# An encoder's instruction planner with a transfer rate of 280 bytes per ns, without table loads in its costs, and with every fifth low part made by GpSimd

## The chip, the cores and the metric

The kernel runs on one core of a Trainium2 chip. The metric is the device time of one launch, in microseconds, as the median of several runs. The engines of the core are TensorE (PE; PEld is its loading of weights), VectorE (DVE), ScalarE (ACT), GpSimd (POOL) and SyncE (SP), which issues nearly all transfers. Each engine executes its own row of instructions in order; semaphores hold an instruction until what it needs is there.

## The reference

Two layers of an encoder over 256 tokens of width 1024, everything in fp32. A layer has four branches, each 256 wide, that are computed from the same normed input, gated, merged and projected, and then a SwiGLU feed-forward part with 2816 hidden columns:

```python
def hybrid_layer(x, mem, ...):
    h = rms_norm(x, norm_mix_g)
    proj = h @ w_in                                   # 1024 x 2304
    rq, rk, rv, rg, pv, nq, nk, nv, mq = jnp.split(proj, 9, axis=-1)
    ret = ...      # retention of rq, rk, rv with rotary and decay both ways, per-head norm, silu(rg)
    pool = ...     # centred means of pv over 2, 4, 8, 16 positions, minus pv, a map per group
    na = ...       # attention of nq, nk, nv in a 2-D window, with bias and normed q and k
    mk, mv = jnp.split(rms_norm(mem, norm_mem_g) @ w_mem_kv, 2, axis=-1)
    mo = ...       # attention of mq to the 256 memory tokens, with normed q and k
    branches = jnp.stack([ret, pool, na, mo], axis=2)
    up = jnp.einsum('bsnc,ncd->bsnd', branches, w_branch)
    gates = jax.nn.sigmoid(h @ w_gate).reshape(b, s, N_BRANCH, dm)
    x = x + jnp.einsum('bsnd,bsnd->bsd', gates, up) @ w_out
    a, g = jnp.split(rms_norm(x, norm_ffn_g) @ w_ffn_in, 2, axis=-1)
    return x + (jax.nn.silu(a) * g) @ w_ffn_out
```

## The kernel before

**Weights.** All weights of both layers are read once, as a stream of 272 slots of 128 x 1024 fp32 (512 KB): per layer 18 for w_in, 4 for the memory's keys and values, 32 for the gates, 8 for the branch projections, 8 for w_out, 44 for the first and 22 for the second feed-forward matrix. A slot j lands in one of four raw buffers (RAW, NR = 4). To keep fp32 precision, it is split in two: the high part whi (ten buffers, NS = 10) is a cast of raw to fp32r by ScalarE, and the low part wlo (ten buffers too) is raw minus whi by VectorE. The activations are split in the same way (hhi and hlo from the normed input, bhi and blo from branches and feed-forward). Each product is then three matmuls on PE: high by high, high by low, low by high. The slots are used in order, each by both token tiles (t = 0 and 1, 128 tokens each), into the PSUM banks A0 to A3 and B0, B1. Banks C0 and C1 (B0 and B1 too in the branches) serve transposes, attention scores and other small steps.

**Transfers.** `issue_dmas` keeps up to four slots under way beyond the number of low parts that have been put in the program; SyncE issues them. So a low part, once placed, is followed in the program by the issue of the slot that reuses its raw buffer.

**The order.** The kernel's rows are not written out by hand. `tile_encoder` runs a planner: each engine is wrapped by `Engine`, whose `call` enters every instruction in a model, `Clock`, before it goes into the program. `Clock.cost` gives an instruction's duration, `Clock.enter` when it starts and ends in the model, transfers included. At each step the planner takes the model's time of PE as now. `background` resumes the chains of small steps (norms, heads, attention, gates, feed-forward's silu: each a Python generator) as soon as what they need is there in the model; `soon`, `ready`, `there`, `need` and `acquire` ask the model's times. `pump` places the casts (`split_hi`) and the low parts (`split_lo`) when the engine is free soon and the transfer has landed in the model, with a window that shrinks with the number of low parts placed ahead of use, WINDOW = (6, 4, 1.5, 0.4) us. `emit` places the matmuls of one slot for one token tile. So a number in the model changes the order of the rows and with it nothing else: what an instruction takes on the chip is not in the program. The first four slots are placed by hand (`begin`).

**The stretches of a layer.** w_in, then four branches in the order neighbourhood attention (2), memory attention (3), retention (0) and pooling (1), each with its 8 gate slots and 2 projection slots; then w_out, then the feed-forward part. `branch_chain` is the one long chain through the four branches: it turns queries and keys into heads (`to_heads`, bank C), computes scores (bank B), the exponentials with their sums (sc, sums), scales, turns and multiplies by the values, while PE works on gate and projection matmuls in between. `ev_nqk` and `ev_mem` norm the heads of queries and keys from the PSUM banks; their reciprocal root is a power on GpSimd of a few elements (sm, rms), otherwise GpSimd has two memsets.

ScalarE computes sigmoids (gates, silu) and exponentials (attention); where one follows the other, a table load stands in its row. VectorE's products of the feed-forward part read `w<-A,rms,w`: bank A, the token's norm, the sigmoid in w.

Nearly every instruction carries the line of the helper that enters it in the model, line 61, so the rows are told apart by tiles. The numbers behind a tile's name in the order's rows are those of buffers.

Of the kernel before, what the change touches and what calls it, by code (L numbers as in the profile page):

```python
# [9 lines left out]
F32 = mybir.dt.float32  # L10
# [20 lines left out]

NS = 10
NR = 4
LEAD = 7
MAX_LAG = 8
WARM = 6.6
TABLE_LOAD = 1.28
WINDOW = (6, 4, 1.5, 0.4)
VERBOSE = False
BRANCHES = (2, 3, 0, 1)  # L40
# [3 lines left out]
class Engine:  # L44
# [5 lines left out]
    def __getattr__(self, op):  # L50
        f = getattr(self.real, op)

        def call(*args, **kw):
            outs = [kw[k] for k in ("out", "accum_out") if kw.get(k) is not None]
            ins = [v for k, v in kw.items() if k not in ("out", "accum_out")]
            rest = list(args)
            if "out" not in kw:
                outs.append(rest.pop(0))
            func = next((v for v in rest if isinstance(v, AF)), None)
            self.clock.enter(self.name, op, outs, [v for v in ins + rest if isinstance(v, bass.AP)], kw, func)  # L60
            return f(*args, **kw)  # L61

        return call


class Clock:
# [5 lines left out]
    def __init__(self):  # L72
        self.at = dict.fromkeys(("PE", "ACT", "DVE", "POOL", "SP", "DMA"), 0.6)
        self.reads, self.writes = {}, {}
        self.mark = 0.0
        self.column = None
        self.narrow = False
        self.table = None

    @property  # L80
    def now(self):
# [2 lines left out]
    def cost(self, eng, op, outs, ins, kw):  # L84
        n = max([x.free_size() for x in outs[-1:] + ins[:1]])
        if eng == "PE":
            o = outs[0]
            n = o.free_size() * (2 if self.now < WARM else 1)
            narrow = op == "matmul" and ins[0].dtype == F32 and o.partition_size() == HD
            change = 0.2 * (narrow != self.narrow)  # L90
            self.narrow = narrow
            if op == "transpose":
                return n * 0.845e-3 + change
            if ins[0].dtype == F32R:
                return n * 0.4167e-3 + 0.0135 + change
            half = o.partition_size() == HD and o.base_partition()
            if o.partition_size() == HD:
                pair, self.column = self.column, None if half else n
                if half and pair == n:
                    return 0.02  # L100
            return max(n, 128) * 1.67e-3 + change
        if eng == "ACT":
            return 0.1 + n * 0.83e-3 + 0.1 * (kw.get("accum_out") is not None) + 0.04 * isinstance(kw.get("scale"), bass.AP)
        if eng == "POOL":
            if op == "memset":
                return 0.1 + n * 1e-3
            return 0.3 + 0.17 * n
        if op in ("tensor_copy", "tensor_scalar", "tensor_scalar_mul", "tensor_scalar_add", "memset"):
            return 0.085 + n * 0.6e-3
        return 0.08 + n * 1.045e-3 + 0.05 * (op == "scalar_tensor_tensor")  # L110

    def span(self, x):
        (stride, parts), *free = x.ap
# [12 lines left out]
        old = [r for r in table.get(key, ()) if r[4] > end - 60 and not (p0 <= r[0] and r[1] <= p1 and lo <= r[2] and r[3] <= hi)]  # L126
        table[key] = old + [(p0, p1, lo, hi, end, eng)]

    def enter(self, eng, op, outs, ins, kw, func=None):
        ins = [x for x in ins if x.space != bass.MemoryType.DRAM]  # L130
        outs = [x for x in outs if x.space != bass.MemoryType.DRAM]
        skip = "PE" if eng == "PE" else None
        t = max([self.last(self.writes, x) + self.LATENCY for x in ins]
                + [self.last(self.reads, x, eng) + self.LATENCY for x in ins if x.space == bass.MemoryType.PSUM]
                + [max(self.last(self.writes, x, skip), self.last(self.reads, x, skip)) + self.LATENCY for x in outs] + [self.at[eng]])
        if func in (AF.Exp, AF.Sigmoid) and func != self.table:
            self.table = func
            self.at["ACT"] += TABLE_LOAD
            t = max(t, self.at["ACT"])
        if op == "dma_start":  # L140
            self.at[eng] = t + 0.45
            t = max(self.at["DMA"], t + 1.2) + (outs + ins)[0].nbytes() / 390e3
            self.at["DMA"] = t
            end = t + 1.0
        else:
            end = self.at[eng] = t + self.cost(eng, op, outs, ins, kw)
        for x in ins:
            self.note(self.reads, x, end, eng)
        for x in outs:
            self.note(self.writes, x, end, eng)  # L150
        self.mark = max(self.mark, end)
# [9 lines left out]
def tile_encoder(ctx: ExitStack, tc: tile.TileContext, a: dict, out: bass.AP):  # L161
# [129 lines left out]
    def split_lo():  # L291
        j = state["lo"]
        for o in HALVES if j < 3 else [slice(None)]:
            nc.vector.tensor_sub(WLO[j % NS][:, o], RAW[j % NR][:, o], WHI[j % NS][:, o].bitcast(F32))
        state["lo"] += 1
        issue_dmas()

    def soon(t, slack=0.4):
        return t <= clock.now + slack

    def pump():
# [5 lines left out]
            window = min(window, 0.8)  # L307
        for _ in range(2):
            j = state["lo"]
            if j < state["hi"] and soon(clock.at["DVE"], window) and soon(clock.last(clock.writes, WHI[j % NS])):  # L310
                split_lo()
            j = state["hi"]
            if (j < min(n_slots, state["free"] + NS, state["lo"] + NR) and soon(clock.at["ACT"], window)
# [868 lines left out]
```

## Time and profile before

| | us |
|---|---|
| runs shown: lowest, median, highest | 842.88, 843.17, 847.2 |
| the profiled execution, whole | 841.89 |
| its span in the trace | 840.0 |
| PE busy | 820.8 |
| VectorE busy | 552.2 |
| ScalarE busy | 470.1 |
| GpSimd busy | 30.5 |

The profiled execution's 841.89 us is its own device time, comparable with the runs; the span of 840.0 is what the trace covers of it, 1.9 less. PE's mean granted clock was 1.00. Stretches of the span, by what PE works on: the start up to about 16 us; the first layer's w_in, gates and branches to about 180; the merge, w_out and the way to the feed-forward part to 265; the feed-forward part to 425; then layer two in the same way, up to 590, 680 and 840. A row of busy time has the engine's share of the span behind it; a row of a wait gives the waiting engine and tile, what released it, microseconds, count and the longest; and a row of the trace has the start in us, the duration in us, the engine, line, operation and operands, and in brackets the idle time ahead of it and what ended that.

### The profile page before, as it was taken

The numbers are of one execution on the slowest core, as the hardware profiler recorded it, in microseconds if no ns is written. First come the engines' busy times: TensorE is split into PE (matmuls) and PEld (weight loads), VectorE is DVE, ScalarE is ACT, GpSimd is POOL, SyncE is SP. The second block draws the span as 40 slices with busy tenths as digits, with TensorE's granted clock in tenths as the row PEclk, the third lists the DMA queues.
The fourth block names the chain that finished last, engine by engine and source line by source line (L and its number), as shares of the span: only waits on it lengthen the run. The fifth ranks groups of instructions, "written<-read, shape, count | busy, mean of one in ns | idle before, by whom it ended". The sixth has DMA issues, their size and how long they took to land.

```text
span 840.0 us, 10795 instructions
## 1 busy us (share of the span) xinstructions
PE 820.8 (98%) x3928; PEld 672.4 (80%) x3928; DVE 552.2 (66%) x802; ACT 470.1 (56%) x726; POOL 30.5 (4%) x32
## 2 busy tenths in 40 slices
PE   8999999999999999999999998999999999999998
PEld 6788778778887888888888877887888878888886
DVE  5898786865677556555568868584775765655541
ACT  6858887445465444444469677754444654444430
POOL 0400100000000000000011001000000000000000
PEclk9999999999999999999999999999999999999999
DMA  8946765546568656566374477446544676666611
GB/s 257 323 140 203 240 199 166 166 147 197 176 180 255 191 180 197 176 198 185 95 220 137 156 246 219 147 126 226 178 157 120 200 228 198 187 187 186 189 52 51
DMA packets 103765, 152.86 MB, mean 182 GB/s; under 512 B 6432, under 2 KB 55328, under 8 KB 103712
## 3 DMA queue, kind: packets, MB, share of 16 engines
q1 hardware_dynamic: 102848, 151.30, 57.1%
q10 hardware_dynamic: 864, 0.88, 0.3%
q8 instruction: 31, 0.51, 0.2%
q14 instruction: 22, 0.18, 0.1%
HBM read 151.10 MB, written 1.05 MB: 181 GB/s over the span
## 4 chain that ended last, share of the span: by engine, by line
PE 78%; ACT 7%; DMA 7%; DVE 6%; issue 2%; POOL 0%; SPq 0%; DVEq 0%; ACTq 0%; POOLq 0%
PE A L61 49%; PE B L61 25%; PE C L61 4%; DVE wlo L61 3%; ACT whi L61 2%; DMA raw<-in_w_in 2%; DMA mem<-in_pool_a 2%; DMA raw<-in_w_ffn_out 1%; DMA raw<-in_w_gate 1%; DVE w L61 1%; ACT rs L61 1%; ACT sc L61 1%; DMA raw<-in_w_mem_kv 1%; ACT qk L61 1%; ACT bhi L61 1%
## 5 line engine op out<-in xcount | busy, mean ns | idle before, releaser
L61 DVE TENSOR_TENSOR wlo<-raw,whi 128x1024 fp32r<-128x1024 f32 (+1 forms) x275 | 330.2, 1212 | 190.9 <-ACT whi L61 190.3
L61 ACT CAST whi<-raw 128x1024 fp32r<-128x1024 f32 (+1 forms) x273 | 284.1, 1050 | 214.0 <-PE A L61 83.0
L61 PE MATMUL A<-whi,hhi 128*128 128x512 f32 (+1 forms) x544 | 213.9, 393 | 1.6 <-ACT whi L61 0.7
L61 PE MATMUL A<-wlo,hhi 128*128 128x512 f32 (+1 forms) x544 | 208.9, 384 | 1.0 <-DVE wlo L61 1.0
L61 PE MATMUL A<-whi,hlo 128*128 128x512 f32 (+1 forms) x544 | 209.1, 384 | 0.0
L61 PEld LDWEIGHTS A<-whi,hhi 128*128 128x128 f32 x544 | 102.3, 188 | 23.2 <-issue 2.6
L61 PEld LDWEIGHTS A<-whi,hlo 128*128 128x128 f32 x544 | 102.2, 188 | 21.2 <-DVE hlo L61 0.8
L61 PEld LDWEIGHTS A<-wlo,hhi 128*128 128x128 f32 x544 | 102.5, 188 | 20.1 <-DVE wlo L61 2.0
L61 PE MATMUL B<-whi,hlo 128*128 128x512 f32 x288 | 112.5, 391 | 0.1
L61 PE MATMUL B<-whi,hhi 128*128 128x512 f32 x288 | 112.3, 390 | 0.0
L61 PE MATMUL B<-wlo,hhi 128*128 128x512 f32 x288 | 112.1, 389 | 0.0
L61 PE MATMUL A<-whi,bhi 128*128 128x512 f32 x272 | 108.3, 398 | 0.0
L61 PE MATMUL A<-whi,blo 128*128 128x512 f32 x272 | 106.2, 390 | 0.0
L61 PE MATMUL A<-wlo,bhi 128*128 128x512 f32 x272 | 106.1, 390 | 0.0
L61 PEld LDWEIGHTS B<-whi,hlo 128*128 128x128 f32 x288 | 54.0, 188 | 12.9 <-DVE hlo L61 1.8
L61 PEld LDWEIGHTS B<-wlo,hhi 128*128 128x128 f32 x288 | 54.1, 188 | 11.3
L61 PEld LDWEIGHTS B<-whi,hhi 128*128 128x128 f32 x288 | 54.1, 188 | 11.0
L61 PEld LDWEIGHTS A<-whi,blo 128*128 128x128 f32 x272 | 51.1, 188 | 11.0
L61 PEld LDWEIGHTS A<-whi,bhi 128*128 128x128 f32 x272 | 51.1, 188 | 10.4 <-issue 0.8
L61 PEld LDWEIGHTS A<-wlo,bhi 128*128 128x128 f32 x272 | 51.2, 188 | 9.7
L61 DVE SCALAR_TENSOR_TENSOR w<-B,rms,w 128x256 f32<-128x256 f32 x72 | 34.7, 482 | 3.9 <-ACT w L61 2.6
L61 ACT CAST bhi<-C 128x512 fp32r<-128x512 f32 x28 | 16.4, 586 | 34.4 <-PE C L61 34.3
(115 smaller groups left out, 605.5 us busy)
## 6 DMA issues: line engine op xcount, KB each, us to landing
raw<-in_w_ffn_in SPq DMA_DIRECT2D x176, 256.0 KB, 3.2
raw<-in_w_gate SPq DMA_DIRECT2D x64, 512.0 KB, 4.4
raw<-in_w_ffn_out SPq DMA_DIRECT2D x44, 512.0 KB, 3.9
raw<-in_w_in SPq DMA_DIRECT2D x35, 512.0 KB, 4.3
raw<-in_w_branch SPq DMA_DIRECT2D x16, 512.0 KB, 4.5
raw<-in_w_out SPq DMA_DIRECT2D x16, 512.0 KB, 4.2
raw<-in_w_mem_kv SPq DMA_DIRECT2D x8, 512.0 KB, 4.3
xn<-in_bias SPq DMA_DIRECT2D x4, 512.0 KB, 5.4
```

The costliest lines, as they stand in the source:

```text
L61: return f(*args, **kw)
```

## The change

The planner's model gets other numbers, and every fifth low part another engine.

- Transfers: 280 in place of 390 bytes per ns, issue 0.48 in place of 0.45 us, 1.1 and 0.9 us of latency before and behind in place of 1.2 and 1.0.
- Table loads: the model had charged ScalarE 1.28 us whenever an exponential followed a sigmoid or the other way round. It no longer does.
- PE: 0.2 us that the model charged between narrow and wide matmuls goes, and a matmul of 512 columns costs 0.216 in place of 0.227 us in the model. VectorE's costs change slightly (1024 elements: 1.145 in place of 1.150 us; a copy of 512: 0.352 in place of 0.392).
- GpSimd: from slot 10 on, the low part of each slot whose number is divisible by five is made by GpSimd (53 of 272), for which the model has 0.3 us + 2.3 ns per element, 2.66 us. `pump` asks GpSimd's time for those in place of VectorE's. They use the wlo buffers 0 and 5 always.

```diff
+POOL_SHARE = 5
...
-TABLE_LOAD = 1.28
...
-            narrow = op == "matmul" and ins[0].dtype == F32 and o.partition_size() == HD
-            change = 0.2 * (narrow != self.narrow)
-            self.narrow = narrow
             if op == "transpose":
-                return n * 0.845e-3 + change
+                return n * 0.84e-3
             if ins[0].dtype == F32R:
-                return n * 0.4167e-3 + 0.0135 + change
+                return n * 0.416e-3 + 0.003
...
-            return max(n, 128) * 1.67e-3 + change
+            return max(n, 128) * 1.67e-3
...
+            if op == "tensor_sub":
+                return 0.3 + n * 2.3e-3
             return 0.3 + 0.17 * n
         if op in ("tensor_copy", "tensor_scalar", "tensor_scalar_mul", "tensor_scalar_add", "memset"):
-            return 0.085 + n * 0.6e-3
-        return 0.08 + n * 1.045e-3 + 0.05 * (op == "scalar_tensor_tensor")
+            return 0.07 + n * 0.55e-3
+        return 0.07 + n * 1.05e-3 + 0.05 * (op == "scalar_tensor_tensor")
...
-        if func in (AF.Exp, AF.Sigmoid) and func != self.table:
-            self.table = func
-            self.at["ACT"] += TABLE_LOAD
-            t = max(t, self.at["ACT"])
         if op == "dma_start":
-            self.at[eng] = t + 0.45
-            t = max(self.at["DMA"], t + 1.2) + (outs + ins)[0].nbytes() / 390e3
+            self.at[eng] = t + 0.48
+            t = max(self.at["DMA"], t + 1.1) + (outs + ins)[0].nbytes() / 280e3
             self.at["DMA"] = t
-            end = t + 1.0
+            end = t + 0.9
...
-            nc.vector.tensor_sub(WLO[j % NS][:, o], RAW[j % NR][:, o], WHI[j % NS][:, o].bitcast(F32))
+            eng = nc.gpsimd if j > 8 and j % POOL_SHARE == 0 else nc.vector
+            eng.tensor_sub(WLO[j % NS][:, o], RAW[j % NR][:, o], WHI[j % NS][:, o].bitcast(F32))
...
-            if j < state["hi"] and soon(clock.at["DVE"], window) and soon(clock.last(clock.writes, WHI[j % NS])):
+            if j < state["hi"] and soon(clock.at["POOL" if j > 8 and j % POOL_SHARE == 0 else "DVE"], window) and soon(clock.last(clock.writes, WHI[j % NS])):
```

What this does to the rows, at three places. First ScalarE's row in the second half of the first layer's memory attention; gt is the gate, sc and sums the attention's exponentials and their sums, whi the casts. Before:

```order
L61 ACTIVATE sc0_119,sums0_151<-B0_65,sums0_151 128x256 x2
L61 CAST whi4_77<-raw0_69 128x1024
L61 ACTIVATE sc1_120,sums1_152<-B1_66,sums1_152 128x256 x2
L61 ACTIVATE sc0_119<-sc0_119,sums0_151 128x256
L61 ACT_TABLE_LOAD
L61 ACTIVATE gt_109<-A0_61,rms_136 128x512
L61 ACTIVATE gt_109<-A2_63,rms_136 128x512
L61 COPY sc0_119<-B0_65 128x512
```

The same place of the changed kernel:

```order
L60 ACT_TABLE_LOAD
L60 ACTIVATE gt_109<-A0_61,rms_136 128x512
L60 ACT_TABLE_LOAD
L60 ACTIVATE sc0_119,sums0_151<-B0_65,sums0_151 128x256 x2
L60 ACT_TABLE_LOAD
L60 ACTIVATE gt_109<-A2_63,rms_136 128x512
L60 ACT_TABLE_LOAD
L60 ACTIVATE sc1_120,sums1_152<-B1_66,sums1_152 128x256 x2
L60 CAST whi5_78<-raw1_70 128x1024
L60 ACTIVATE sc1_120<-sc1_120,sums1_152 128x256
```

The two gates now stand between the two pairs of exponentials, with a table load at each turn: four loads where one stood. In the whole row there are 16 in place of 10.

Second, VectorE's row on the way into the first layer's feed-forward part: wlo are the low parts, w3 the product with the sigmoid, blo the low parts of the activations. Before:

```order
L61 TENSOR_TENSOR blo0_101<-C0_67,bhi0_97 128x512
L61 TENSOR_TENSOR wlo5_88<-raw1_70,whi5_78 128x1024
L61 TENSOR_TENSOR wlo6_89<-raw2_71,whi6_79 128x1024
L61 SCALAR_TENSOR_TENSOR w3_128<-A2_63,rms_136,w3_128 128x256 x2
L61 TENSOR_TENSOR wlo7_90<-raw3_72,whi7_80 128x1024
```

Changed:

```order
L60 TENSOR_TENSOR blo0_101<-C0_67,bhi0_97 128x512
L60 TENSOR_TENSOR wlo4_87<-raw0_69,whi4_77 128x1024
L60 SCALAR_TENSOR_TENSOR w3_128<-A2_63,rms_136,w3_128 128x256 x2
L60 TENSOR_TENSOR wlo6_89<-raw2_71,whi6_79 128x1024
L60 TENSOR_TENSOR blo1_102<-C1_68,bhi1_98 128x512
```

The product now stands ahead of the low part wlo6, and wlo5 is gone from this row. On ScalarE's row the cast whi6 has moved behind the sigmoid in the same way.

Third, GpSimd's row in the first layer's branches; sm and rms are the powers. Before:

```order
L61 TENSOR_TENSOR sm8_146<-sm7_145,mhalf_137 128x4
L61 TENSOR_TENSOR rms_136<-sm9_147,mhalf_137 128x1
L61 TENSOR_TENSOR rms_136<-sm10_148,mhalf_137 128x1
L61 TENSOR_TENSOR sm0_138<-sm11_149,mhalf_137 128x4
```

Changed:

```order
L60 TENSOR_TENSOR sm8_146<-sm7_145,mhalf_137 128x4
L60 TENSOR_TENSOR sm10_148<-sm9_147,mhalf_137 128x4
L60 TENSOR_TENSOR wlo0_83<-raw2_71,whi0_73 128x1024
L60 TENSOR_TENSOR rms_136<-sm11_149,mhalf_137 128x1
L60 TENSOR_TENSOR rms_136<-sm0_138,mhalf_137 128x1
L60 TENSOR_TENSOR wlo5_88<-raw3_72,whi5_78 128x1024
```

Low parts stand between the powers, which GpSimd does in order. Its row goes from 36 to 89 instructions, VectorE's from 650 to 598 lines of this listing. PE has the same matmuls in another order, mainly in the branches; in the feed-forward parts its order hardly changes.

More of the change, by code (lines that the diff above doesn't have):

```diff
@@ L58, in call @@
                 outs.append(rest.pop(0))
-            func = next((v for v in rest if isinstance(v, AF)), None)
-            self.clock.enter(self.name, op, outs, [v for v in ins + rest if isinstance(v, bass.AP)], kw, func)
+            self.clock.enter(self.name, op, outs, [v for v in ins + rest if isinstance(v, bass.AP)], kw)
             return f(*args, **kw)
@@ L76, in __init__ @@
         self.column = None
-        self.narrow = False
-        self.table = None
     @property
@@ L127, in note, with enter @@
         table[key] = old + [(p0, p1, lo, hi, end, eng)]
-    def enter(self, eng, op, outs, ins, kw, func=None):
+    def enter(self, eng, op, outs, ins, kw):
         ins = [x for x in ins if x.space != bass.MemoryType.DRAM]
```

## The prediction

> **What bounds the kernel now.** I read the page's busy times first, then busy time by stage, then what TensorE (PE) waited for, and last the rows around those waits.
>
> ```profile
> PE 820.8 (98%) x3928; PEld 672.4 (80%) x3928; DVE 552.2 (66%) x802; ACT 470.1 (56%) x726; POOL 30.5 (4%) x32
> ```
>
> TensorE is busy for 820.8 of 840.0 us; VectorE (DVE), ScalarE (ACT) and GpSimd (POOL) have room on average. The same by stage (columns: PE, PEld, DVE, ACT, POOL, clock, DMA share, GB/s):
>
> ```profile
> 16.00:180.00 164.00, 159.33 (x821) 129.47 (x820) 127.86 (x212) 120.31 (x203) 14.19 (x11) 1.00 0.62 202
> 180.00:265.00 85.00, 83.28 (x385) 68.37 (x384) 58.46 (x82) 43.87 (x67) 1.11 (x2) 1.00 0.61 190
> 265.00:425.00 160.00, 160.00 (x728) 132.44 (x727) 92.51 (x113) 72.54 (x94) 0.55 (x1) 1.00 0.58 179
> 425.00:590.00 165.00, 159.61 (x827) 129.84 (x826) 121.11 (x192) 115.35 (x198) 12.28 (x10) 1.00 0.56 181
> 590.00:680.00 90.00, 89.00 (x410) 73.08 (x409) 61.55 (x86) 47.05 (x71) 1.11 (x2) 1.00 0.58 176
> 680.00:840.00 160.00, 156.26 (x707) 128.98 (x705) 82.95 (x100) 61.19 (x74) 0.00 (x0) 1.00 0.50 155
> ```
>
> In the feed-forward stretch 265 to 425 PE is never idle. Idle is 4.7 us in the first layer's branches (16 to 180), 1.7 on the way to its feed-forward part, 5.4 and 1.0 in the same places of layer two, and 3.7 at the end (the store). So a better order can win at most 4.7 + 1.7 + 5.4 + 1.0 = 12.8 us; a worse one has no such floor. The clock is 1.00 throughout. What PE waited for:
>
> ```profile
> PE C L61 <- DVE w L61: 7.6, 5, 3.0
> PE C L61 <- DVE blo L61: 1.8, 2, 1.6
> PE B L61 <- DMA mem<-in_pool_a: 1.8, 3, 1.1
> ```
>
> These ten waits are 11.2 us. All are steps of the attention, norm or feed-forward chain that stand in PE's row a little before their operand is ready; waits for weights themselves are under 2 us.
>
> **The change, part by part.** PE's matmuls are the same in number; only their order moves. The pace of a row of matmuls:
>
> ```profile
> 288.36 10.88 PE B L61 x48
> ```
>
> 10.88 / 48 = 0.227 us each.
>
> *Slower transfers in the planner.* A weight cast (whi) is now placed later in ScalarE's row, and its subtraction (wlo) later in VectorE's. Both engines work in order, so a cast whose transfer has not landed holds up what stands behind it. That happens here:
>
> ```profile
> 259.74 1.05 ACT L61 CAST whi<-raw 128x1024 fp32r<-128x1024 f32 x1 [1.66 <-DMA raw<-in_w_ffn_out]
> 260.69 0.47 ACT L61 ACTIVATE w<-A,rms 128x256 f32<-128x256 f32 x1
> 260.82 1.23 DVE L61 TENSOR_TENSOR wlo<-raw,whi 128x1024 fp32r<-128x1024 f32 x1 [1.49 <-ACT whi L61]
> 261.96 1.00 DVE L61 SCALAR_TENSOR_TENSOR w<-A,rms,w 128x256 f32<-128x256 f32 x2
> 263.01 0.44 PE L61 MATMUL C<-ident_gain,w 128*128 128x128 f32 x2 [1.68 <-DVE w L61]
> 676.94 0.33 PE L61 MATMUL C<-ident_gain,w 128*128 128x128 f32 x1 [0.96 <-DVE w L61]
> ```
>
> The cast waits for the transfer, the sigmoid behind it starts late, VectorE's product waits behind that slot's wlo, and PE waits 1.68 us; the same place in layer two costs 0.96. In the new order that slot's cast and wlo stand behind the sigmoid and the product. Both waits should go: -2.6 us. What is late next is that slot's wlo, which PE does not need for several slots.
>
> The memory keys show the same thing twice:
>
> ```profile
> 94.16 1.05 ACT L61 CAST whi<-raw 128x1024 fp32r<-128x1024 f32 x1 [0.98 <-DMA raw<-in_w_gate]
> 100.08 0.30 PE L61 MATMUL C<-ident_gain,w 128*128 128x128 f32 x1 [1.32 <-DVE w L61]
> 101.07 0.52 PE L61 MATMUL C<-ident_gain,w 128*128 128x128 f32 x3 [0.69 <-DVE w L61]
> 505.56 1.05 ACT L61 CAST whi<-raw 128x1024 fp32r<-128x1024 f32 x1 [1.63 <-PE A L61]
> 514.73 0.52 PE L61 MATMUL C<-ident_gain,w 128*128 128x128 f32 x3 [2.99 <-DVE w L61]
> ```
>
> Ahead of the evictions stands a cast that waits 0.98 us for its transfer in layer one and 1.63 us for PE to release its buffer in layer two. Fewer casts stand ahead now, so the evictions come about that much sooner, and a little more by the cast itself: I take 1.3 of the 2.0 us in layer one and 1.8 of the 2.99 in layer two, -3.1 us (0 to 5.0). The start and the pooling step:
>
> ```profile
> 36.50 0.33 PE L61 MATMUL C<-ident_gain,w 128*128 128x128 f32 x1 [1.58 <-DVE blo L61]
> 582.63 0.78 PE L61 MATMUL B<-mem,qk 128*64 128x136 f32 x12 [1.08 <-DMA mem<-in_pool_a]
> 583.88 0.77 PE L61 MATMUL B<-mem,qk 128*64 128x136 f32 x12 [0.47 <-DMA mem<-in_pool_a]
> ```
>
> The query and key transposes move 21 matmuls (4.8 us) later in PE's row, which covers the 1.58 us; but slot 10, GpSimd's first, is then needed earlier, and I give 1.0 us back. The pooling matmuls of layer two move by the same 21 matmuls, past a wait of 1.08 + 0.47 = 1.55. Together -2.1 us. SyncE's row keeps its transfers but for five places where a bias, mem, rgb or weight transfer passes another; none of these is among the late ones above, so I cost them at nothing.
>
> *Table loads that the planner no longer sees.* ScalarE's row now has 16 instead of 10.
>
> ```profile
> L61 ACT ACT_TABLE_LOAD x10 | 12.8, 1283 | 1.3 <-PEq L1171 1.2
> L61 ACT ACTIVATE gt<-A,rms 128x512 f32<-128x512 f32 x32 | 21.7, 688 | 9.9 <-PE A L61 9.8
> L61 ACT ACTIVATE sc<-B,sums 128x256 f32<-128x256 f32 x16 | 7.4, 471 | 1.0 <-DVE sums L61 0.9
> L61 ACT ACTIVATION_READ_ACCUMULATOR sc<-B,sums 128x1 f32 x16 | 3.2, 200 | 0.0
> L61 ACT CAST whi<-raw 128x1024 fp32r<-128x1024 f32 x271 | 282.8, 1054 | 213.0 <-PE A L61 83.0 <-PE B L61 72.9 <-issue 22.6
> ```
>
> The six added ones cost between 0 (all behind PE's matmuls) and 6 x 1.28 = 7.7 us. Four stand in one stretch, the second half of the first layer's memory attention. From the end of the gate in A0, ScalarE has gate 0.69, load 1.28, two exponentials (2 x 0.67), load 1.28, gate 0.69, load 1.28, two exponentials 1.34, cast 1.05, and a scaling like an exponential 0.47: 9.4 us at most, 8.8 with the small overlaps that back-to-back rows show. PE has 30 matmuls and four transposes there before it needs that result: 30 x 0.227 + 0.4 = 7.2. It waits 1.6 us. In layer two the same sum with two added loads gives 1.0. I take +2.6.
>
> *Every fifth low part on GpSimd.* 53 subtractions leave VectorE.
>
> ```profile
> L61 DVE TENSOR_TENSOR wlo<-raw,whi 128x1024 fp32r<-128x1024 f32 x269 | 326.2, 1223 | 189.7 <-ACT whi L61 189.0
> L61 POOL MEMSET rl<- 64x512 f32 x2 | 1.0, 518 | 0.3 <-POOLq L1171 0.3
> 34.60 0.55 POOL L61 TENSOR_TENSOR rms<-sm,mhalf 128x1 f32<-128x1 f32 x1
> 37.97 1.49 POOL L61 TENSOR_TENSOR rms<-sm,mhalf 128x1 f32<-128x1 f32 x1 [2.82 <-DVE sm L61]
> 37.82 1.23 DVE L61 TENSOR_TENSOR wlo<-raw,whi 128x1024 fp32r<-128x1024 f32 x1
> ```
>
> VectorE loses 53 x 1.22 = 65 us of busy time. No such subtraction on GpSimd is in the trace. The nearest row is the memset, 1.0 ns per element of one stream: 1.04 us for 1024 elements at the least, and 3.1 if two reads and a write pass one after the other. I take the middle, 2.1, which is 53 x 2.1 = 111 us on an engine that has 810 free. [...]
>
> What decides is who waits for whom. The last three rows show that a small power took 1.49 instead of 0.55 us: it started while a wlo ran on VectorE (37.82 to 39.05) and ended 0.41 us behind it. GpSimd is held by a VectorE instruction that reads two operands from SBUF; the other direction the trace cannot show, as GpSimd's reads here are of a few elements. If it does not exist, VectorE gains 65 us of room and PE nothing, for VectorE is not the bound. If it does, each of the 53 can hold VectorE, and all its in-order row, for 2.1 us. 35 of them fall outside the two branch stages, where casts wait for PE to release buffers (the cast row: 83.0 + 72.9 us of such waits), so the weights are ahead and it costs nothing; the raw buffer freed about 1 us later is covered by the same lead. The 18 in the branch stages cost between 0 and 18 x 2.1 = 38 us. I take +3: one in three meets a step that PE is about to need, and delays it by half a microsecond after the room in PE's row. [...]
>
> *The sum.* The profiled execution took 841.9 us (span 840.0 and 1.9 around it). -2.6 - 3.1 - 2.1 + 2.6 + 3.0 = -2.2: 839.7. The runs shown have their median 1.3 above that execution, so I forecast **841 us**. Half a per cent, 4.2 us, is about what can be told from no change.
>
> **Rivals.** *Faster: the gains without the prices.* Table loads and GpSimd's share hide in the other engines' room, -7.8 us, or up to the 12.8 of all idle: 830 to 836, and 835 likeliest. For it: the planner's transfers are later than real ones almost everywhere, which leaves steps more room than before. Against it: the four loads in a row, worked out above.
>
> *Slower: GpSimd holds VectorE.* In the branch stages VectorE is busy 127.9 of 164 us, so a wlo is usually queued when GpSimd starts. If half of the 18 meet a waiting step and each passes 1.2 us on to PE, that is +10.8 in place of +3: 849; it decides from about 9 us on. For it: the held power above, and that the planner books no such wait. Against it: ScalarE, not VectorE, ends most waits of wlo (189 us).
>
> *Slower: all six table loads show.* +7.7 in place of +2.6: 846, still within the half per cent. A change that does nothing is excluded, as the rows of four engines differ.
>
> **How the numbers follow.** Forecast, with the table-load rival in it (839 to 847): 0.45. Faster rival: 0.26. GpSimd rival, above 847.4: 0.29. 834 and 851 leave about one in ten on either side: 834 is all gains and no prices with something to spare, 851 the GpSimd rival with its price at 1.4 us. The likeliest case alone has 839 to 847.
>
> **What would show it.** Right: PE's waits for w in the C banks fall from 7.6 to about 3 us; no wait near the first feed-forward transposes; 16 table loads with a PE wait of 1 to 2 us near 130 us; VectorE busy near 487; GpSimd near 140. Wrong: wlo on VectorE that last longer than 1.22 us or start late with GpSimd as releaser, PE waits of over a microsecond at scores and transposes between 40 and 180 us, or any PE idle time in 265 to 425.

## The result

The changed kernel takes 850.88 us in the median of 7 runs (848.35 to 854.18), the kernel before 843.17 (7 runs, 842.33 to 847.2): a ratio of 1.0083, 95% interval 1.0056 to 1.011. It is slower by 0.8%, where I had forecast no change, a little on the fast side. Of my cases it is nearest the rival in which GpSimd holds VectorE (849). The profiled execution took 849.28 us (span 847.3), 7.4 more than that of before.

The busy times and three stretches of the profile after (columns as in the prediction):

```profile
PE 826.9 (98%) x3928; PEld 675.5 (80%) x3928; DVE 521.2 (62%) x754; ACT 476.9 (56%) x727; POOL 160.5 (19%) x85
16.00:180.00 164.00, 156.70 (x781) 126.14 (x780) 127.34 (x201) 123.21 (x202) 37.45 (x21) 1.00 0.62 202
265.00:425.00 160.00, 160.00 (x730) 132.46 (x729) 81.08 (x103) 74.27 (x96) 27.86 (x13) 1.00 0.61 184
425.00:590.00 165.00, 158.26 (x788) 128.90 (x787) 117.87 (x183) 115.13 (x193) 38.35 (x21) 0.98 0.55 176
```

PE does the same 3928 matmuls, but is busy 6.1 us longer. About 2 us of that are matmuls at a lower granted clock (0.98 in the mean of layer two's branches); the rest is spread over short stalls and is not followed further here. In the first layer's branches PE is idle 2.6 us more. The feed-forward stretch has no idle time, as before. VectorE was busy for 521 us where I expected 487, so its instructions last longer: I had taken off 65 us for 53 low parts, and 31 came off. What PE waited for:

```profile
PE C L60 <- DVE w L60: 7.2, 5, 4.2
PE B L60 <- DVE sc L60: 2.5, 1, 2.5
PE B L60 <- DVE rl L60: 1.3, 2, 1.0
PE A L60 <- DVE gt L60: 0.8, 1, 0.8
```

The waits at feed-forward entry, the start and the pooling transfers are gone or shorter; one wait for w has grown from 3.0 to 4.2 us, and one for sc is new. The two transposes at the feed-forward entries, which had waited 1.68 and 0.96 us, now follow without a wait:

```profile
260.19 0.60 PE L60 MATMUL C<-ident_gain,w 128*128 128x128 f32 x4
677.55 0.60 PE L60 MATMUL C<-ident_gain,w 128*128 128x128 f32 x4
```

**GpSimd holds VectorE.** The following rows are from layer two's memory keys: VectorE, PE and GpSimd in the trace after (L60), and in the last row VectorE's same product before (L61):

```profile
517.82 2.34 POOL L60 TENSOR_TENSOR wlo<-raw,whi 128x1024 fp32r<-128x1024 f32 x1
517.88 2.31 DVE L60 TENSOR_SCALAR sm<-sm,rms 128x4 f32<-128x4 f32 x1 [0.90 <-POOL sm L60]
520.30 0.42 DVE L60 TENSOR_TENSOR w<-A,sm 128x256 f32<-128x256 f32 x1
520.87 0.88 PE L60 MATMUL C<-ident_gain,w 128*128 128x128 f32 x3 [4.16 <-DVE w L60]
521.97 0.63 PE L60 MATMUL A<-wlo,hhi 128*128 128x512 f32 x1
522.39 0.63 PE L60 MATMUL A<-whi,hlo 128*128 128x512 f32 x1
513.83 0.23 DVE L61 TENSOR_SCALAR sm<-sm,rms 128x4 f32<-128x4 f32 x1 [0.90 <-POOL sm L61]
```

A product of four elements takes 2.31 instead of 0.23 us: it starts 0.06 us after GpSimd's low part and ends 0.03 us behind it. PE's wait for w is 4.16 us, where it was 2.99. Behind it the matmuls follow each other in 0.42 us instead of 0.23: that is the lower clock (0.50 from 518.85 to 525.67 us). Which instructions are held shows at two other places. GpSimd's low part runs from 50.06 to 52.44 beside products of VectorE, and another one from 215.76 on beside a sum of two SBUF operands, which stands once more, without GpSimd, at 219.36:

```profile
50.06 2.38 POOL L60 TENSOR_TENSOR wlo<-raw,whi 128x1024 fp32r<-128x1024 f32 x1 [8.15 <-ACT whi L60]
50.53 1.40 DVE L60 SCALAR_TENSOR_TENSOR w<-A,rms,rope 128x512 f32<-128x512 f32 x2
215.76 2.41 POOL L60 TENSOR_TENSOR wlo<-raw,whi 128x1024 fp32r<-128x1024 f32 x1 [8.24 <-ACT whi L60]
216.24 2.48 DVE L60 TENSOR_TENSOR xn<-xn,gt 128x512 f32<-128x512 f32 x1
219.36 0.69 DVE L60 TENSOR_TENSOR xn<-xn,gt 128x512 f32<-128x512 f32 x1
```

The products that read a PSUM bank (A) take 1.40 us for two under GpSimd's low part; one alone took 0.74 us in the trace before, so they are not held. The sum of two SBUF tiles takes 2.48 instead of 0.69. In the whole trace 19 of VectorE's instructions are longer for this reason, by 29 us together (their durations less those of their like), all with operands in SBUF alone, none in the feed-forward part of layer one. Not every such instruction is held: a product of one element at 254.68 us and a reciprocal of two at 491.43 started under a low part of GpSimd too and took 0.22 and 0.16 us, as without it. The traces show a hold in both directions: VectorE's product took 2.31 in place of 0.23 us here, and GpSimd's power 1.49 in place of 0.55 us in the trace before.

GpSimd's own price was 2.45 us each, where I had taken 2.1:

```profile
L60 POOL TENSOR_TENSOR wlo<-raw,whi 128x1024 fp32r<-128x1024 f32 x53 | 130.1, 2454 | 513.5 <-ACT whi L60 489.8
```

**Table loads.** The four loads of the first layer's memory attention, and PE's wait behind them:

```profile
125.06 1.28 ACT L60 ACT_TABLE_LOAD   x1
126.35 0.69 ACT L60 ACTIVATE gt<-A,rms 128x512 f32<-128x512 f32 x1
127.05 1.28 ACT L60 ACT_TABLE_LOAD   x1
129.38 1.28 ACT L60 ACT_TABLE_LOAD   x1
130.67 0.69 ACT L60 ACTIVATE gt<-A,rms 128x512 f32<-128x512 f32 x1
131.37 1.28 ACT L60 ACT_TABLE_LOAD   x1
134.41 0.30 PE L60 MATMUL B<-ident_gain,sc 128*128 128x128 f32 x1 [2.52 <-DVE sc L60]
```

PE waited 2.52 us at 134 us where I had worked out 1.6.

### The profile page after: what moved, and what is told of

The parts are those of the page before. It is cut to its first block, busy times and chain, and to the rows that moved or that the text cites. A ratio compares the mean times of both kernels' runs of the same rounds, so it can differ in the third digit from the quotient of the medians.

```text
span 847.3 us, 10834 instructions
## 1 busy us (share of the span) xinstructions
PE 826.9 (98%) x3928; PEld 675.5 (80%) x3928; DVE 521.2 (62%) x754; ACT 476.9 (56%) x727; POOL 160.5 (19%) x85
## 4 chain that ended last, share of the span: by engine, by line
PE 71%; issue 5%; DVE 5%; POOL 1%; ACT 1%; DMA 1%; DVEq 0%; ACTq 0%; POOLq 0%
PE A L60 43%; PE B L60 25%; PE C L60 3%; DVE wlo L60 1%; DVE w L60 1%; POOL sm L60 1%; ACT whi L60 1%; DMA raw<-in_w_branch 1%; POOL wlo L60 1%; DVE mem L60 1%; DVE sm L60 0%; DVE gt L60 0%; DVE xn L60 0%; ACT gt L60 0%; DVE ls L60 0%
## 5 line engine op out<-in xcount | busy, mean ns | idle before, releaser
L60 ACT CAST whi<-raw 128x1024 fp32r<-128x1024 f32 (+1 forms) x273 | 283.7, 1049 | 200.2 <-PE A L60 78.5
L60 DVE TENSOR_TENSOR wlo<-raw,whi 128x1024 fp32r<-128x1024 f32 (+1 forms) x222 | 269.8, 1226 | 180.1 <-ACT whi L60 179.0
L60 POOL TENSOR_TENSOR wlo<-raw,whi 128x1024 fp32r<-128x1024 f32 x53 | 130.1, 2454 | 513.5 <-ACT whi L60 489.8
L60 PE MATMUL A<-whi,hhi 128*128 128x512 f32 (+1 forms) x544 | 215.4, 396 | 1.5 <-DVE gt L60 0.8
L60 PE MATMUL A<-whi,hlo 128*128 128x512 f32 (+1 forms) x544 | 210.3, 387 | 0.0
L60 PE MATMUL A<-wlo,hhi 128*128 128x512 f32 (+1 forms) x544 | 210.1, 386 | 0.2 <-DVE wlo L60 0.2
L60 PEld LDWEIGHTS A<-whi,hhi 128*128 128x128 f32 x544 | 103.2, 190 | 22.5 <-issue 2.2
L60 PEld LDWEIGHTS A<-whi,hlo 128*128 128x128 f32 x544 | 102.9, 189 | 21.4 <-DVE hlo L60 0.8
L60 PEld LDWEIGHTS A<-wlo,hhi 128*128 128x128 f32 x544 | 103.3, 190 | 19.5 <-DVE wlo L60 1.5
L60 PE MATMUL B<-whi,hlo 128*128 128x512 f32 x288 | 112.3, 390 | 0.1
L60 PE MATMUL B<-whi,hhi 128*128 128x512 f32 x288 | 112.3, 390 | 0.0
L60 PE MATMUL B<-wlo,hhi 128*128 128x512 f32 x288 | 112.1, 389 | 0.0
L60 PE MATMUL A<-whi,bhi 128*128 128x512 f32 x272 | 108.5, 399 | 0.2 <-ACT gt L60 0.2
L60 PE MATMUL A<-whi,blo 128*128 128x512 f32 x272 | 106.2, 390 | 0.0
L60 PE MATMUL A<-wlo,bhi 128*128 128x512 f32 x272 | 106.1, 390 | 0.0
L60 PEld LDWEIGHTS B<-whi,hlo 128*128 128x128 f32 x288 | 54.1, 188 | 12.1 <-DVE hlo L60 0.9
L60 PEld LDWEIGHTS B<-wlo,hhi 128*128 128x128 f32 x288 | 54.1, 188 | 11.2
L60 PEld LDWEIGHTS B<-whi,hhi 128*128 128x128 f32 x288 | 54.1, 188 | 11.1
L60 PEld LDWEIGHTS A<-whi,bhi 128*128 128x128 f32 x272 | 51.1, 188 | 12.0 <-issue 1.7
L60 PEld LDWEIGHTS A<-whi,blo 128*128 128x128 f32 x272 | 51.1, 188 | 11.0
L60 PEld LDWEIGHTS A<-wlo,bhi 128*128 128x128 f32 x272 | 51.2, 188 | 9.7
L60 DVE SCALAR_TENSOR_TENSOR w<-B,rms,w 128x256 f32<-128x256 f32 x72 | 34.8, 483 | 14.4 <-ACT w L60 13.1
```

## The experiments

All times are medians; ratios are to the kernel before, timed on the same chip in the same rounds. The clock is the mean that was granted to PE in a run, as the median over the runs; it differs from run to run of one kernel (the kernel before: 0.989 to 1.000), and the longer runs are mostly those with the lower clock (of the changed kernel the shortest, 848.35 us, had 0.996 and the longest, 854.18, had 0.989). The experiments were run in five groups, each on another chip, and the kernel before itself had medians from 842.5 to 844.3 us in them. So a difference between runs of two groups is known to one or two microseconds only; where it matters, the difference of the ratios is given too.

**First, the two suspects in the changed kernel's order.** The low parts back to VectorE at the same places of the program:

```diff
+            if j > 8 and j % POOL_SHARE == 0:
+                clock.enter("POOL", "tensor_sub", ...)   # the planner still reckons GpSimd
+                tc.nc.vector.tensor_sub(*args)
```

> The changed kernel's rows on every engine, but the 53 low parts stand at their places in VectorE's row instead of GpSimd's (the planner still reckons them as GpSimd's, so nothing else moves). Theory A (GpSimd's low parts hold VectorE, and the wait that grows from it costs PE its clock): PE's wait in layer two's memory keys falls from 4.16 us to between 2.1 and 3.3, the granted clock stays 1.00 in every run, and the time falls by 4 to 7 us against the changed kernel: 844 to 847, a ratio to the kernel before of 1.001 to 1.005. Theory B (the new order, table loads above all, costs the time, whoever makes the low parts): within 1 us of the changed kernel, ratio 1.007 or more, and the 2.7 us wait at the memory attention of layer one stays.

Measured: 843.62 us, ratio 0.9997 (0.9972 to 1.0023). So -7.3 us against the changed kernel with no other row moved, a little more than theory A had: the hold is real and costs seven microseconds. The wait at the memory attention stayed (2.54 us), as theory B has it, and the clock did not stay at 1.00 (0.995): here the wait at the memory keys was 2.19 us, and slow matmuls followed that too.

One low part left out:

```diff
+            if j == 170:
+                clock.enter("POOL", "tensor_sub", ...)
+                continue
```

> The changed kernel without one subtraction: the low part of slot 170, the one that GpSimd makes while VectorE's small product for layer two's memory keys takes 2.31 instead of 0.23 us. Its buffer keeps old values. Theory A: that product is short again, PE's wait there is 2.0 to 2.2 instead of 4.16 us, and the granted clock is 1.00 in all runs, so 2.1 us of wait and 2 to 5 us of slow matmuls go: ratio to the kernel before 1.001 to 1.004. If the clock falls for another reason than this wait, it is 0.99 to 0.996 still and the ratio is about 1.006.

Measured: 848.35 us, ratio 1.0053 (1.0027 to 1.0079). The product is short again and the wait halved:

```profile
519.94 0.23 DVE L60 TENSOR_SCALAR sm<-sm,rms 128x4 f32<-128x4 f32 x1 [0.90 <-POOL sm L60]
520.84 0.87 PE L60 MATMUL C<-ident_gain,w 128*128 128x128 f32 x3 [2.33 <-DVE w L60]
```

That is 2.5 us off the median for one instruction, near the 1.8 us of wait, though the two intervals overlap (the changed kernel's ratio begins at 1.0056). The clock was 0.996 and not 1.00 in all runs, so this wait was not the only cause of its fall.

Empty work on PE in that wait:

```diff
+                    if fill and bank is C[1] and (r, t) == (0, 1):
+                        for _ in range(fill):            # fill = 24 in layer two
+                            tc.nc.tensor.transpose(B[0][:, 0:P], ident, ident)
```

> The changed kernel with 24 extra transposes of the identity (about 2.7 us of PE time into an unused bank) placed on PE just ahead of the transpose that waits 4.16 us in layer two's memory keys. The wait's end is not touched. If PE's idle time is what lowers the granted clock: clock 1.00 in all runs, PE's idle time there about 1.4 us, the transposes end at the same time, and only the slow matmuls go, 2 to 5 us: ratio to the kernel before 1.003 to 1.006. If the clock falls for another reason (load, GpSimd's work): clock 0.99 to 0.996 and ratio 1.008 as before.

Measured: 850.73 us, ratio 1.0078 (1.0052 to 1.0103), clock 0.996. The profiled execution had no slow matmuls at all, a clock of 1.000 and 846.84 us, but the median did not move. A wait of 1.8 us (from start to start) was left there. This settles nothing; longer waits are filled below.

No table changes inside the branches; four loads are left:

```diff
-        nc.scalar.activation(g, ps, AF.Sigmoid, scale=RH[t])
+        nc.scalar.activation(g, ps, AF.Exp, scale=RH[t])
```

(and the same in the retention branch).

> The changed kernel with an exponential in place of the sigmoid in the gates and the retention branch (other values, the same instructions), so that no table changes inside the branches: 4 to 6 table loads instead of 16. Theory B: the 2.7 and 0.6 us waits of PE in layer one's memory attention go nearly, -3 to -5 us: ratio to the kernel before 1.003 to 1.005. Theory A: under 1.5 us, since the low part on VectorE that took 3.43 us there, held by GpSimd, stands on the same chain: ratio 1.007.

Measured: 840.28 us, ratio 0.996 (0.994 to 0.9981): -10.6 us, more than either theory had. Both suspects out at once (the two diffs together):

> The changed kernel's order with both suspects out: the 53 low parts at their places in VectorE's row, and an exponential in place of the sigmoid in gates and retention (4 table loads, other values). So far: the changed kernel 850.9, low parts on VectorE 843.6, no tables 840.3. If the two are all that the new order costs: 832 to 835, like the kernel without the share (833.1). If both took away the same waits: 838 to 841. If the order itself is bad: above 841.

Measured: 831.76 us, ratio 0.9848 (0.9819 to 0.9878), at the lower end of the first case. So 850.9 falls by 7.3 without the hold, by 10.6 without the loads, by 19.1 without both (7.3, 10.4 and 19.8 by the ratios): two causes, nearly additive.

**Second, the parts of the change one by one.** Only the transfers, on the kernel before:

```diff
-            self.at[eng] = t + 0.45
-            t = max(self.at["DMA"], t + 1.2) + (outs + ins)[0].nbytes() / 390e3
+            self.at[eng] = t + 0.48
+            t = max(self.at["DMA"], t + 1.1) + (outs + ins)[0].nbytes() / 280e3
...
-            end = t + 1.0
+            end = t + 0.9
```

> The kernel before with nothing but the four transfer numbers of the change (280 bytes per ns and the latencies): 12 table loads. The gains that I predicted at the feed-forward entry and the memory keys come from these numbers: 836 to 841, ratio 0.992 to 0.998, with no wait over 0.5 us at 263 us and 677 us. If a later cast only moves the waits elsewhere: ratio 0.999 to 1.002.

Measured: 835.77 us, ratio 0.9905 (0.9879 to 0.9931). The slower transfers in the planner win 7 to 8 us (the medians differ by 6.8, the ratio is 0.95% of 843). The time is just below the expected range, and one part of the expectation's reason failed: the feed-forward entries were as expected, but at the memory keys of layer two a wait of 2.6 us stayed.

Everything but GpSimd's share (split_lo and pump ask VectorE alone):

> The changed kernel's planner with its numbers, but no low part on GpSimd, in the planner or on the chip: 12 table loads. Theory A: the cost is gone, 842 to 845, ratio 0.998 to 1.002. If the slower transfer numbers and the unseen table loads cost time of themselves: ratio 1.003 to 1.006.

Measured: 833.09 us, ratio 0.9872 (0.9845 to 0.9899), 9 us below either expectation. It is 2.7 us below transfers_only in the same group, so the unseen table loads and the smaller costs of PE and VectorE together lose nothing.

The share alone, on the kernel before:

```diff
+            if j > 8 and j % 5 == 0:
+                clock.enter("DVE", "tensor_sub", ...)   # the planner still reckons VectorE
+                tc.nc.gpsimd.tensor_sub(*args)
```

> The kernel before with the 53 low parts made by GpSimd at the same places of the program (the planner still reckons them as VectorE's, so every other row is that of before). Theory A (GpSimd's hold on VectorE is the cost, in any order): slower than before by 4 to 9 us, ratio 1.005 to 1.011, with several VectorE instructions of SBUF operands at 2 us and more. Theory C (the hold costs only in the new order, where more table loads take the slack): within 2 us of before, ratio 1.000 to 1.002.

Measured: 854.38 us against 842.52 of the kernel before in that group, ratio 1.013 (1.009 to 1.017), with a clock of 0.989. This is beyond theory A's range. Its trace has 17 held instructions of VectorE, the same product among them (2.33 us), and PE waits of 3.0 and 2.4 us with slow matmuls behind both.

The loads seen by the planner again, the share kept (the lines removed by the change put back):

> The changed kernel with the 1.28 us per table change in the planner again; GpSimd keeps its share. There are 16 table loads all the same, at other places. My prediction's step (the planner no longer sees the loads, +2.6 us) says -2 to -4 us against the changed kernel: ratio 1.003 to 1.006. Theory A says that the loads' cost comes with the share, so that little is won: ratio 1.006 to 1.010.

Measured: 838.51 us, ratio 0.9939 (0.9915 to 0.9963), 12.4 us below the changed kernel (12.1 by the ratios), though 16 loads stand in it too. That is more than either theory had.

The same planner without the share:

> The changed kernel's numbers with the table loads in the planner and without GpSimd's share: 16 table loads stand in ScalarE's row, against 12 without them in the planner. If what the planner sees helps also without the share: 828 to 832. If it only helped since it moved the loads away from a held VectorE: 832 to 836.

Measured: 836.34 us, ratio 0.9899 (0.9875 to 0.9923), at the upper end of the second case. Here the share, with the order that it brings, costs 2.2 us (3.4 by the ratios), against 17.8 with the loads unseen. And the planner's sight of the loads, worth 12.4 us with the share, loses 3.2 without it (836.3 against 833.1; 2.3 by the ratios, whose intervals overlap). The number of held instructions does not tell the cost: 19 in the changed kernel (29 us longer together), 17 in share_on_before (26 us) and 18 in tables_seen (31 us).

Loads without the share:

> The kernel without GpSimd's share and with 4 table loads instead of 12 (exponential in place of the sigmoid, other values). Theory D (a table load is cheap while VectorE is not held; the share makes the loads dear, by place and by hold): -0 to -3 us against the kernel without the share, 830 to 833. If a load costs what the changed kernel lost by them (10.6 us for 12 loads, 0.9 each): -7 us, 826.

Measured: 828.78 us, ratio 0.9808 (0.9783 to 0.9834): 4.3 us for 8 loads (5.4 by the ratios), where the changed kernel lost 10.6 by 12. Neither end of the expectation held.

GpSimd's low parts in the feed-forward slots alone, on no_share (`j % 136 >= 70 and j % 5 == 0`):

> The kernel without the share, in which the 27 low parts of the feed-forward slots whose number is divisible by five are made by GpSimd all the same, at the same places of the program. Theory A: VectorE's instructions there read PSUM or have slack, so the hold costs nothing: within 1 us of the kernel without the share, 832 to 835, no PE idle time in the feed-forward stretches. If GpSimd's share costs by its number of low parts, wherever they are: 27 of 53 of 17.8 us, 842.

Measured: 832.33 us, ratio 0.9849 (0.9824 to 0.9875), as without the share. 27 of these instructions cost nothing there. Beside them start 37 instructions of VectorE, of which 29 read a PSUM bank, and three were held, by 2.3 us together. The two feed-forward stretches of this kernel, with PE's busy time of 165.00 and 184.96 us (columns as above):

```profile
250.00:415.00 165.00, 165.00 (x754) 136.46 (x753) 86.98 (x111) 77.42 (x102) 27.50 (x13) 1.00 0.62 186
640.00:825.00 185.00, 184.96 (x841) 152.82 (x840) 91.42 (x119) 81.25 (x105) 29.58 (x13) 1.00 0.55 168
```

The next table shows where PE lost time in these kernels. For each matmul the time to the next one's start beyond the median of its form is taken from the trace and summed over the same amount of work (us; slow matmuls are in it). Each column is one execution.

| stretch | before | changed | vector_same_order | no_tables | vector_no_tables | no_share | tables_seen |
|---|---|---|---|---|---|---|---|
| layer 1: to neighbourhood attention | 2.5 | 2.4 | 2.5 | 1.8 | 2.5 | 5.6 | 1.4 |
| memory keys | 3.6 | 1.4 | 2.1 | 0.5 | 0.3 | 0.1 | 1.5 |
| memory attention | -0.1 | 5.7 | 3.8 | 0.3 | -0.1 | -0.1 | 0.6 |
| retention, pooling | 1.7 | 2.8 | 1.4 | 2.8 | 1.4 | 1.3 | 1.4 |
| merge, w_out | 0.8 | 1.2 | 0.5 | 1.2 | 0.5 | 0.5 | 1.2 |
| feed-forward entry | 2.0 | 0.1 | 0.6 | 0.1 | 0.1 | 0.1 | 0.1 |
| layer 2: w_in | 1.2 | 2.4 | 1.4 | 2.4 | 1.3 | 0.1 | 1.7 |
| to memory keys | 3.0 | 6.4 | 3.8 | 5.2 | 0.5 | 0.6 | 5.9 |
| memory attention, retention | 0.4 | 1.0 | 2.5 | 0.3 | 0.3 | 0.3 | 1.5 |
| pooling | 2.7 | 2.0 | 0.9 | 2.0 | 1.0 | 1.0 | 1.3 |
| feed-forward entry | 1.6 | 0.5 | 0.5 | 0.4 | 0.4 | 0.4 | 0.4 |
| all, with the rest | 24.0 | 31.2 | 25.5 | 22.0 | 12.9 | 14.4 | 22.3 |

The memory attention of layer one loses by the loads (5.7 to 0.3) and less by the hold (5.7 to 3.8). Layer two's memory keys lose by both: 5.2 with the hold alone, 3.8 with the loads alone, 0.5 with neither. In retention, merge and w_out, and in layer two's w_in and pooling, it is the hold alone that makes the difference.

**Third, the clock.** Long waits made on purpose in no_share, at the memory keys of both layers, by copies of a small table onto itself on VectorE; then the same with PE filled by transposes:

```diff
+        for _ in range(delay):                   # 20 or 7, token tile 1 only
+            tc.nc.vector.tensor_copy(rope, rope)
```

> The kernel without GpSimd's share, with 20 copies of the rotary table onto itself (about 4.4 us of VectorE) ahead of the last product for the memory keys, in both layers, so that PE waits some 4 us more at each of the two transposes. Theory E (a wait of about 4 us costs PE its clock): slow matmuls after both waits, a granted clock of 0.994 to 0.997 in the median against 0.998, and 1 to 3 us more than the two waits add. Otherwise the clock is 0.998 to 1.000 and the time is that of no_share plus the two waits, about 841 to 842.

> As wait_4, but PE does 28 transposes of the identity into an unused bank (about 3 us) ahead of each of the two waiting transposes, so that it idles for about a microsecond there. The transposes' operand is as late as in wait_4. Theory E: the clock is 0.998 to 1.000 and the time 1 to 3 us below wait_4. If idle time doesn't lower the clock: the same clock and time as wait_4.

> As wait_4 (7.0 and 8.0 us of wait at the memory keys of the two layers), with 60 empty transposes (about 6.5 us) in place of 28. Idle time left: 0.5 and 1.4 us. If idle time lowers the clock: no slow matmuls after the two places, a granted clock of 0.997 to 1.000 in the median against 0.990, and 846 to 847.5 us, 2.5 to 4 below wait_4 (849.9). If the late operand or the place does it: 0.990 and 849 to 850.

> As wait_4 with 7 copies in place of 20, so that PE waits about 2.5 us in layer one and 3.2 in layer two. If any wait of that length costs the clock: 0.993 to 0.995 in the median, and 841 to 843 us. If it depends on more than the length (the waits of 2.2 to 3.2 us in the traces so far went both ways): runs between 838.5 (833.1 and the added 4.8 to 5.5 us) and 842, with clocks from 0.994 to 1.000.

Measured:

- wait_4: 849.92 us (1.0074, 1.005 to 1.0098), clock 0.990. The waits came out at 7.0 and 8.0 us, longer than expected, since each copy took about 0.33 us of VectorE's row.
- wait_4_filled: 848.52 us (1.0053, 1.0031 to 1.0075), clock 0.992, with 4.0 and 4.8 us of idle time left; too little was filled.
- wait_filled_60: 843.06 us (0.9997, 0.9983 to 1.0011), clock 1.000. The clock is as expected, the time is below the range.
- wait_3: 837.78 us (0.9939, 0.9921 to 0.9958), clock 0.997, a little below either range. In its trace both waits were 2.8 us long and slow matmuls followed both.

Two stretches with the waits, wait_4 first, then wait_filled_60 (the clock is the third column from the end):

```profile
100.00:110.00 10.00, 3.13 (x10) 2.62 (x10) 9.29 (x26) 3.46 (x6) 0.00 (x0) 0.76 0.27 79
515.00:530.00 15.00, 7.14 (x27) 5.68 (x26) 13.32 (x30) 5.04 (x7) 1.53 (x1) 0.66 0.39 119
...
100.00:110.00 10.00, 9.68 (x72) 8.79 (x71) 9.36 (x23) 3.81 (x6) 0.00 (x0) 1.00 0.28 86
515.00:530.00 15.00, 14.79 (x90) 12.92 (x89) 14.43 (x26) 8.26 (x11) 0.00 (x0) 1.00 0.46 143
```

The operand is 7.0 us late in layer one in both kernels, and 8.0 and 6.9 us late in layer two. The empty transposes lift the clock in these stretches from 0.76 and 0.66 to 1.00, and the slow matmuls are gone: PE's idle time lowers its clock. The time falls by 6.9 us. Not all of this is clock: in the traces the slow matmuls behind the two waits of wait_4 cost 2.5 and 2.3 us beyond the usual pace, and the rest is the shorter delay in layer two and a difference of 1.0 us ahead of the first place.

**A kernel that beats both.** The sigmoid written as half of one plus a hyperbolic tangent, which stands in ScalarE's row beside the exponentials without a load (in the trace exponentials from 78.87, a gate from 79.36 and exponentials from 79.93 us):

```diff
-        nc.scalar.activation(g, ps, AF.Sigmoid, scale=RH[t])
+        nc.scalar.activation(g, ps, AF.Tanh, scale=RG[t])        # RG is half of RH
...
-            nc.vector.tensor_mul(g, ps, g)
+            nc.vector.scalar_tensor_tensor(out=g, in0=g, scalar=1.0, in1=ps, op0=ALU.add, op1=ALU.mult)
...
+                nc.vector.scalar_tensor_tensor(out=o, in0=A[2 * t + blk], scalar=0.5, in1=o, op0=ALU.mult, op1=ALU.add)
...
```

(and in the same way in the retention branch; RG is made by one more small product.)

> The kernel without GpSimd's share, with the sigmoids of gates and retention written as half of one plus a hyperbolic tangent (which needs no other table than the exponential: 4 table loads), the one added in VectorE's product, the half in the residual's addition. Right values. From no_share_no_tables: 828 to 831, ratio to the kernel before 0.982 to 0.986.

Measured: 829.44 us, ratio 0.9841 (0.9811 to 0.987): 1.6% below the kernel before, 4 table loads. The transfers win 7 to 8 us of it, the other numbers of the planner about 3 (835.8 to 833.1), the missing loads about 4 (833.1 to 829.4).

## Why the prediction failed

**Slower transfers (-2.6, -3.1 and -2.1 us): right in sum and at five of six places.** transfers_only won 7 to 8 us where I had a sum of 7.8. In the changed kernel the feed-forward entries lost 1.9 and 1.1 us less, the first layer's memory keys 2.2, the pooling of layer two 0.7, and the wait at the start fell from 1.58 to 0.47. The sixth place failed: layer two's memory keys, where I had -1.8. In transfers_only 2.6 of the 2.99 us stayed, so fewer casts ahead did not shorten this wait; in the changed kernel it grew by 1.2 us, as the hold and a table load came to it.

**GpSimd's low parts (+3.0): the step that failed.** I had 18 of them in the branches, and one in three passing half a microsecond on to PE. The hold, with the order kept, costs 7.3 us in the changed kernel, 8.5 in the same order with no loads, and 11.9 in the order of before. The bounds were there, and the mechanism was a rival; what was mis-sized is "one in three meets a step that PE is about to need, and delays it by half a microsecond", six delays in all. In the trace after, 32 low parts start outside the feed-forward stretches (20 of them in the branches), and 19 instructions of VectorE are held, 1.5 us each; the 7.3 us are 0.4 for each of them. So the price of one was near my half microsecond, and the number was three times too small. The one that was taken out alone, a product of 0.23 us in the chain of the memory keys, waited the whole 2.3 us, and PE waited for what follows it. I had weighed ScalarE's casts, which end most waits of the low parts, and not the chain of small steps.

The sum itself had a second flaw. It added the share and the loads as separate terms, +5.6 us together, and left out that the share's order changes what the loads cost: 10.6 us in this order, 4.3 without the share. Measured from no_share, the share costs 17.8 us, and only 7 to 8.5 of that are the hold.

**Table loads (+2.6): too small, and with the wrong reason.** I put them down to the planner's blindness. no_share is blind too, has 12 loads and is the fastest of the planner's orders with sigmoids; tables_seen sees them and has 16. Nor do the four loads in layer one's memory attention come from the blindness: tables_seen_no_share, which sees the loads and has no share, has four there too (123.12, 125.10, 127.44 and 129.43 us), while no_share has four in the neighbourhood attention instead. What makes the planner put them there stays open. The loads cost 10.6 us in the changed kernel's order, and I had worked out two of the places. The memory keys of layer two were not among them. There a load at 497.65 us stands ahead of four casts and of the keys' evictions; without the loads PE loses 0.5 us there instead of 3.8 (the table's columns with the low parts on VectorE).

**The clock: not in the prediction at all.** The median clock is 0.994 in the changed kernel, 0.995 to 0.998 in five sets of runs of before, and 0.998 in no_share. In the profiled execution the 4.16 us wait was followed by 4.5 us of slow matmuls, which took 2.3 us more than at the usual pace.

The sum: I forecast -7.8 us for the transfers and +5.6 for loads and share. Measured are -10.1 us by all numbers of the planner (843.2 to 833.1) and +17.8 us by the share. Step by step, the 17.8 are 8.5 for the hold, some 6 for the loads that its order makes dear (10.6 less the 4.3 that loads cost without it), and about 3 for the order itself (831.8 against 828.8, with neither hold nor loads). These steps join runs of several groups, so each is known to one or two microseconds. What is not settled is how much of each is clock: the traces show one execution of each kernel, and the clock differs between runs.

## What to carry to other kernels

An engine with little work can still be a dear place for more: here GpSimd was busy for 30 of 840 us, and its low parts cost 7 to 12 us, as they held VectorE. Ask of each instruction moved to GpSimd which VectorE instruction with SBUF operands alone may start beside it (all 19 that were held in the changed kernel had such operands), and who waits for that one. Work for GpSimd belongs where VectorE mostly reads PSUM and PE does not wait for it (27 low parts in the feed-forward slots cost nothing, with 29 of the 37 VectorE instructions beside them reading PSUM). And when a planner gets several new numbers at once, try each alone: here the transfers won 1% and the share, with the order that it brought, lost 2%, and together they looked like a small loss.

## What the runs showed of the hardware

**PE's clock falls after short waits.** The waits here are counted from start to start, less the usual pace. After waits of 3.8 to 8.0 us (seven in these traces) the matmuls were slow each time, 6 to 11 of them at 0.42 us each, up to 3.6 to 5.8 us after PE resumed, and not longer for the longer waits. The lower clock begins within the wait: in the changed kernel it is 0.50 over these 6.8 us, of which PE stood idle for the first two, until 520.87:

```profile
518.85:525.67 6.82, 4.80 (x13) 3.96 (x14) 6.58 (x8) 3.65 (x6) 1.31 (x1) 0.50 0.67 209
```

After waits of 2.0 to 3.3 us it went both ways: 3.15 us at the memory keys of before was followed by none, 2.34 us in vector_same_order by seven, 2.24 us in no_share by four. In wait_3 both waits of 2.8 us were enough. What decides it at these lengths was not shown.

**Where a held instruction ends.** A held instruction of VectorE ends 0.03 us (four elements, 0.23 us long by itself) to 1.08 us (a low part, 1.22 us long by itself) behind GpSimd's, whatever its start: the four held low parts of the changed kernel started 0.45 to 2.35 us ahead of GpSimd's end and all ended 1.08 to 1.09 us behind it, and the six held sums of xn and gt ended 0.55 or 0.56 us behind, of 0.69 by themselves. GpSimd's low parts took 2.45 us in the mean.
